# Attention's products with V as float32 products in one half of TensorE's columns

## The chip, the cores and the metric

One core of a Trainium2 chip runs the whole program. The metric is the device time of one execution in microseconds (us), median of three runs. The engines are TensorE (PE; its weight loads are listed as PEld), VectorE (DVE), ScalarE (ACT), GpSimd (POOL) and SyncE (SP), which issues most transfers.

## What is computed

Two layers of a hybrid block over 1152 tokens (1024 latent ones and 128 of context). In each layer three mixers share an input and an output projection: grouped-query attention (GQA, 6 heads), latent attention (MLA, 4 heads) and a state-space part; a squared-ReLU feed-forward part follows. The change is in the attention of both kinds:

```python
def block_attention(q, k, v, scale):
    ...
    def one_block(qblk):
        s = jnp.einsum('bqgrd,bsgd->bgrqs', qblk, k).astype(F32) * scale
        pr = jax.nn.softmax(s, axis=-1).astype(v.dtype)
        return jnp.einsum('bgrqs,bsgd->bqgrd', pr, v)
```

Heads have 64 values. A latent query reads 1152 keys (128 context keys from the cache, then its own 1024); a context query reads the 128 context keys of the request.

## The kernel before

Almost every product is made of float32r operands that are split in a high and a low part: `cp` rounds the high part (ACT), `lo` subtracts it to give the low part (DVE, or POOL for weights), and `mm` (line 69) multiplies the parts in two or three products that are added in PSUM. `tr` (line 73) transposes on TensorE.

`attn` streams 30 groups in each layer, one for each head of a block of 384 queries: 12 of MLA (three blocks, four heads), then 18 of GQA (three blocks, six heads). Blocks 0 and 1 hold three latent query tiles (`nq` = 3). Block 2 holds two latent tiles and the context tile, so its groups have nine key tiles for 256 queries and a tenth, `j` = 9, for the 128 context queries. For a group the steps are:

- `score`: scores `S` of a query tile against a third of the keys (three products for MLA, two for GQA); DVE copies them to `P` and takes the maximum (line 788), ACT makes the exponentials over 1152 keys (line 97).
- `trans`: three transposes of `P` to `pt` in PSUM, keys on the partitions; ACT rounds them to `ph` (line 65), DVE subtracts to give `pl` (line 78).
- `prod`: the stationary operand `g.V(j)` is the key tile's V, its high part in columns 0 to 63 and its low part in 64 to 127. Two products, with `ph` and then `pl` as the moving operand of 384 (or 256, or 128) columns, add to `oT` [128, 384].
- `fin1` copies `oT` to `oS`; `fin2` transposes `oS` and adds its two halves, which joins the products of V's high and low parts.

The scores of the next group are written between the products of this one. Beside this stream, `pull` issues background work at fixed points: the state-space outputs (`ssm_b`), the keys and values of GQA (`kv_gqa`, whose values are split by ACT and POOL to `VY`), the modulation (`mods`), the output projection (`out_proj`). The framework's scheduler then sets the order in each engine's queue, so the order in the source isn't the order on the engine. TensorE takes its queue in order.

One place of the kernel before already has float32 products in a part of the array: `mods` puts four products of different k side by side, 32 columns each and 512 columns of moving data (tile `m`, moving operand `raw`, stationary `cT`), in layer 0 beside GQA. A float32 product shows as two rows of MATMUL and two of LDWEIGHTS in the trace, a float32r product as one of each.

Of the kernel before, what the change touches and what calls it, by code (L numbers as in the profile page):

```python
# [4 lines left out]
F32 = mybir.dt.float32  # L5
# [8 lines left out]
L = 2  # L14
NT = 9            # token tiles: 8 latent, 1 context
NB = 3            # blocks of three token tiles
BK = 384
EPS = 1e-6
# how long (ns) background work is left alone where a chain over several engines is under way
# [3 lines left out]
# worth (ns) of background work issued at each point of the main stream  # L23
PU = (600, 850, 600, 500, 1100, 500, 400, 400, 500, 900)
SEG = [[(0, 384, 0)], [(0, 384, 0)], [(0, 256, 0), (256, 384, 1)]]
# columns of the packed small parameters
# [4 lines left out]
class Group:  # L31
    """One head of one block of queries in the attention stream."""
# [5 lines left out]
class Net:  # L38
# [7 lines left out]
    # ---------------------------------------------------------------- helpers  # L46
# [9 lines left out]
    # Rough prices (ns) of what is issued, so that background work can be paced.  # L56
# [42 lines left out]
    def rsqrt(self, v, n):  # L99
        """1/sqrt of v [128, n], by Newton's steps in float32."""  # L100
# [29 lines left out]
    # Work that runs beside the main stream: generators, advanced a step at a time.  # L130
    # One that yields a number is left alone for about so many ns.
# [7 lines left out]
    def turns(self, gens):  # L139
        """Advances the generators in the list in turn; more may be added to it meanwhile."""  # L140
        due = {}
        while gens:
            ready = [g for g in gens if due.get(g, 0) <= self.now]
            if not ready:
                g = min(gens, key=lambda g: due[g])
                yield due[g] - self.now
                ready = [g]
            for g in ready:
                try:
                    due[g] = self.now + (next(g) or 0)  # L150
                except StopIteration:
                    gens.remove(g)
                yield

    def pull(self, ns=500):
        """Issues background work worth ns of the engine that it uses most."""
# [15 lines left out]
    # ------------------------------------------------------------- modulation  # L172
    def mods(self, l, groups, engs=None, raw=None, ps=None):
        """Columns of the modulation: at the start as products, later on VectorE, with a product
        that only sums over the partitions."""
        nc = self.nc
        sums = []
        for g in groups:
# [16 lines left out]
            elif l == 0 and g < 10:  # L195
                # four products of different k side by side in the array, 32 columns each, of which two count
# [59 lines left out]
    # ------------------------------------------------------------------ norms  # L256
# [3 lines left out]
    def squares(self, sq, src, h, dve=False, eng=None):  # L260
        """Squares of the h-th quarter of src, over 1024; their sum over the features of a partition
        is in sq[:, 0] after the last one."""
# [11 lines left out]
    def stats(self, sq, out, src=None, pool=None, tag="m", bufs=2):  # L274
        """Broadcast of rsqrt(mean(src^2) + eps) over features, [128, 384] in PSUM; without src,
        the squares are there."""
# [21 lines left out]
    def prenorm(self, l, which, x, b, hi, lo, sq, squared=False):  # L298
        """x (overwritten) -> modulated h, split in hi + lo; without sq, x is normed already."""
# [19 lines left out]
    def postnorm(self, l, which, src, x, b, sq, squared=False, again=False, lazy=False):  # L319
        """x += gate * gain * rmsnorm(src); src is overwritten. again: sq gets the squares of x.  # L320
        lazy: it isn't waited for, and GpSimd does what it can."""
# [28 lines left out]
    # ------------------------------------------------------------------ build  # L350
    def build(self):
# [16 lines left out]
        # silu of the conditioning, split  # L368
        # (what follows the conditions only keeps 32 columns in reach)
# [61 lines left out]
    # ---------------------------------------------------------------- in-proj  # L431
    def in_proj(self, l, hT):
# [54 lines left out]
        # ---- group 3: kpe | z | dt  # L487
# [12 lines left out]
        # ---- x, B, C of the state-space part: feature-major, with the convolution  # L500
# [27 lines left out]
        # the first two blocks before the last one, whose norm may still be under way  # L528
# [49 lines left out]
        # ---- group 2: va | qc | kvc, and the query up-projection of MLA  # L578
# [63 lines left out]
        # ---- group 1: qa | ka; its first products run ahead of what is left of group 2  # L642
# [38 lines left out]
    def rope(self, x, C, S, nh, q, tp, eng, eng2=None):  # L681
        """x [128, nh*d] in place: x*C + partner(x)*S, d = 4q."""
# [15 lines left out]
    def ssm_steps(self, l, b, tp):  # L698
        """Softplus of the steps of a block, cumulated decays; everything [128, dir, tile, head]."""
# [19 lines left out]
        # dA = -exp(a_log) * dt  # L719
# [35 lines left out]
    # -------------------------------------------------------------- attention  # L755
    def dup_split(self, pt, hi, lo, n):
        """pt rows (x; x): hi and lo in full."""
        self.cp(hi[:, :n], pt[:, :n])
        self.lo(lo[:, :n], pt[:, :n], hi[:, :n])

    def attn(self, groups, tp, ps):
        """Streams the groups: scores of the next one run beside the products with V of this one.
        A group has b, prep() -> pairs of (stationary [128, 384], moving [128, 1280]),
        V(j) -> [128 keys, (hi | lo)], scale, dst() and done()."""
# [8 lines left out]
        def score(g, i, j):  # L773
            """Scores of query tile i against the j-th third of the keys, with their maximum."""
# [28 lines left out]
        def trans(g, j):  # L803
# [6 lines left out]
            ph = tp.tile([128, BK], R, name="ph", bufs=3)  # L810
            pl = tp.tile([128, BK], R, name="pl", bufs=3)
            self.cp(ph[:, c0:c1], pt[:, c0:c1])
            self.lo(pl[:, c0:c1], pt[:, c0:c1], ph[:, c0:c1])
            return ph[:, c0:c1], pl[:, c0:c1], c0, c1

        def prod(g, j, t):
            ph, pl, c0, c1 = t
            if j == 0:
                g.oT = ps.tile([128, BK], F32, name="oT", bufs=1)
            first, last = j in (0, 9), j in (8, 9)  # L820
            self.mm(g.oT[:, c0:c1], g.V(j), ph, first, False)
            self.mm(g.oT[:, c0:c1], g.V(j), pl, False, last)

# [23 lines left out]
        for n, g in enumerate(groups):  # L847
# [3 lines left out]
            for j in range(nj):  # L851
# [4 lines left out]
                prod(g, j, ts[j])  # L856
# [11 lines left out]
    def qT(self, src, tp, ps, name):  # L868
        """src: three [128 tokens, 128] tiles -> split transposes."""
# [8 lines left out]
    # ------------------------------------------- the three mixers  # L878
    def mix(self, l):
        """MLA (beside it the state-space outputs, then keys and values of GQA), then GQA  # L880
        (beside it the out-projection of the blocks that are done)."""
# [9 lines left out]
        # ---- keys and values of MLA  # L891
# [38 lines left out]
        V = xm.tile([128, 10, 4, 2, 64], R, name="V")  # L930
        for j in range(10):
# [6 lines left out]
            self.cp(V[:, j, :, 0, :], p3)  # L938
            self.lo(V[:, j, :, 1, :], p3, V[:, j, :, 0, :])
# [20 lines left out]
        VY = kv.tile([128, 10, 2, 2, 64], R, name="VY")  # L960
        KY = kv.tile([128, 2, 1280], R, name="KY")
        self.bg += [self.kv_gqa(l, VY, KY, ss, blk), self.ssm_b(l, ss)]

        def query(src, h, n, rep, col):
            """Head h of the block at hand, n columns repeated rep times: [128, 3, rep * n]."""
# [10 lines left out]
        for b in range(NB):  # L976
            for h in range(4):
# [22 lines left out]
                groups.append(Group(b, prep, lambda j, h=h: V[:, j, h].rearrange("p v d -> p (v d)"),  # L1000
# [10 lines left out]
        for b in range(NB):  # L1011
            for h in range(6):
# [33 lines left out]
                groups.append(Group(b, prep, lambda j, h=h: VY[:, j, h // 3].rearrange("p v d -> p (v d)"),  # L1046
# [41 lines left out]
    def ssm_a(self, l, ss):  # L1088
        """Per chunk: its state, and beside it the decayed scores (keys on the partitions)."""
# [18 lines left out]
        def front(t):  # L1108
            """The products of B and C of the chunk, both groups."""
# [524 lines left out]
```

## Time and profile before

| | |
|---|---|
| median of three runs | 3523.4 us |
| lowest and highest | 3520.69 and 3524.45 us |
| span of the profiled execution, first to last instruction | 3515.7 us |
| between span and median | 7.7 us |
| attention of layer 0, of layer 1 | about 407 to 882 us, 2160 to 2610 us |
| PE busy, DVE busy, ACT busy (share of the span) | 92%, 68%, 44% |

The attention takes about a quarter of the time. A busy engine is one that has at least one instruction under way: a matmul's duration includes its way through the array, and the next one starts long before it ends. What a matmul takes from its successors is therefore read from start to start, not from its duration. For DVE and ACT durations count.

### The profile page before, as it was taken

What the parts mean: (1) busy time and instruction counts of PE and PEld (TensorE: products, weight loads), DVE (VectorE), ACT (ScalarE), POOL (GpSimd) and SP (SyncE); (2) the same over time, 40 slices, a digit from 0 to 9 for tenths busy, and PEclk for the clock granted to TensorE, in tenths of its full rate; (3) what the DMA queues carried; (4) which work ended last, traced back from release to release, by engine and by line L of the source; (5) the groups of instructions that cost most, each with busy time, mean ns of one, the idle gap of its engine ahead of it and who ended that gap; (6) DMA issues with size and microseconds to landing.
All of it is one profiled execution on the core that took longest, in us unless ns stands there. A gap on an engine that the chain in (4) does not pass through costs nothing.

```text
span 3515.7 us, 51450 instructions
## 1 busy us (share of the span) xinstructions
PE 3229.9 (92%) x18578; PEld 3044.7 (87%) x18578; DVE 2400.3 (68%) x6199; ACT 1559.8 (44%) x3250; POOL 1279.6 (36%) x918
## 2 busy tenths in 40 slices
PE   6978799999799999999989778999887999999997
PEld 3966698788699999999989667989887999999997
DVE  7887898766666787784588878997758433333336
ACT  4454577766442211112444646787654412222223
POOL 5356432134651112112564553341446422222135
PEclk8989899999899999999999889999998999999998
DMA  5253323512322333332433533231223211111133
GB/s 205 80 172 108 113 72 107 184 49 96 125 93 82 96 96 98 95 91 78 139 120 102 169 105 108 81 98 61 80 98 103 79 49 42 43 43 43 40 105 132
DMA packets 164532, 340.77 MB, mean 97 GB/s; under 512 B 14429, under 2 KB 105909, under 8 KB 160693
## 3 DMA queue, kind: packets, MB, share of 16 engines
q1 hardware_dynamic: 161012, 335.32, 30.0%
q8 instruction: 146, 2.39, 0.3%
q10 hardware_dynamic: 3264, 2.16, 0.2%
q14 instruction: 110, 0.89, 0.1%
HBM read 280.99 MB, written 56.44 MB: 96 GB/s over the span
## 4 chain that ended last, share of the span: by engine, by line
PE 71%; DVE 20%; ACT 3%; DMA 3%; issue 2%; POOL 1%; SPq 0%; DVEq 0%; ACTq 0%; POOLq 0%
PE g L69 47%; PE S L69 5%; PE op L69 5%; PE oT L69 4%; PE pt L73 4%; DVE big L89 2%; PE m L69 2%; DVE rs_t L83 2%; PE m L73 2%; DVE cv L93 1%; DVE big L83 1%; DVE E L93 1%; DVE P L788 1%; DVE h L83 1%; DVE pl L78 1%
## 5 line engine op out<-in xcount | busy, mean ns | idle before, releaser
L78 POOL TENSOR_TENSOR w<-raw,w 128x1024 fp32r<-128x1024 f32 (+1 forms) x266 | 653.1, 2460 | 1409.3 <-ACT w L65 1365.8
L69 PE MATMUL g<-h,w 128*128 128x384 f32 x5328 | 953.6, 339 | 14.3 <-DVE h L78 12.9
L69 PEld LDWEIGHTS g<-h,w 128*128 128x128 f32 x5328 | 931.8, 189 | 17.7 <-DVE h L78 13.9
L69 PE MATMUL g<-big,w 128*128 128x384 f32 x4608 | 818.7, 336 | 13.7 <-DVE big L78 9.9
L69 PEld LDWEIGHTS g<-big,w 128*128 128x128 f32 x4608 | 800.6, 188 | 19.4 <-DVE big L78 12.0
L65 ACT CAST w<-raw 128x1024 fp32r<-128x1024 f32 (+1 forms) x266 | 275.9, 1041 | 651.6 <-PE g L69 366.1
L83 DVE TENSOR_TENSOR big<-big,g 128x384 f32<-128x384 f32 x336 | 182.9, 551 | 289.2 <-PE g L69 288.5
L83 DVE TENSOR_TENSOR r<-r 128x384 f32<-128x384 f32 x192 | 146.6, 765 | 294.3 <-ACT r L97 294.1
L69 PE MATMUL g<-w,h 128*128 128x512 f32 (+1 forms) x1296 | 320.9, 404 | 24.0 <-ACT w L65 6.1
L788 DVE TENSOR_SCALAR_CACHE_REDUCE P<-S 128x384 f32<-128x384 f32 (+1 forms) x500 | 265.9, 541 | 101.7 <-PE S L69 95.8
L69 PEld LDWEIGHTS g<-w,h 128*128 128x128 f32 x1296 | 255.7, 200 | 70.2 <-DVE h L78 6.9
L78 DVE TENSOR_TENSOR pl<-pt,ph 128x384 fp32r<-128x384 f32 (+2 forms) x560 | 270.2, 498 | 40.1 <-ACT ph L65 35.2
L65 ACT CAST ph<-pt 128x384 fp32r<-128x384 f32 (+2 forms) x560 | 233.1, 444 | 90.6 <-PE pt L73 77.6
L73 PE MATMUL pt<-cst,P 128*128 128x128 f32 x1460 | 256.1, 275 | 1.3 <-ACT P L97 0.9
L97 ACT ACTIVATE r<-g 128x384 f32<-128x384 f32 x192 | 94.3, 491 | 362.1 <-PE g L69 344.7
L93 DVE SCALAR_TENSOR_TENSOR macc<-raw,cT,macc 128x128 f32<-128x128 f32 x784 | 254.9, 389 | 0.0
L69 PE MATMUL op<-big,w 128*128 128x384 f32 x1152 | 227.1, 343 | 8.4 <-DVE big L78 8.4
L78 DVE TENSOR_TENSOR big<-r,big 128x384 fp32r<-128x384 f32 x192 | 167.7, 874 | 86.7 <-ACT big L65 86.3
L97 ACT ACTIVATE P<-P,mx 128x1152 f32<-128x1152 f32 x180 | 210.5, 1170 | 27.9 <-DVE mx L89 27.0
L69 PEld LDWEIGHTS op<-big,w 128*128 128x128 f32 x1152 | 202.8, 191 | 9.9 <-DVE big L78 9.0
L73 PEld LDWEIGHTS pt<-cst,P 128*128 128x128 f32 x1460 | 188.3, 142 | 16.8 <-issue 1.7
L65 ACT CAST big<-r 128x384 fp32r<-128x384 f32 x192 | 98.2, 512 | 185.4 <-DVE r L83 185.2
(299 smaller groups left out, 4933.9 us busy)
## 6 DMA issues: line engine op xcount, KB each, us to landing
raw<-in_w SPq DMA_DIRECT2D x176, 512.0 KB, 3.6
raw<-in_w_mod SPq DMA_DIRECT2D x80, 512.0 KB, 3.5
raw<-in_w_out SPq DMA_DIRECT2D x48, 512.0 KB, 3.6
big<-s_x SPq DMA_DIRECT2D x13, 1536.0 KB
E<-s_ac SPq DMA_DIRECT2D x36, 384.0 KB, 4.3
s_x<-big SPq DMA_DIRECT2D x9, 1536.0 KB
cv<-s_cv SPq DMA_DIRECT2D x36, 320.0 KB, 3.5
h<-in_w_mod SPq DMA_DIRECT2D x16, 512.0 KB, 9.2
```

The costliest lines, as they stand in the source:

```text
L65: self.nc.scalar.copy(out, in_)
L69: self.nc.tensor.matmul(out, lhsT=lhsT, rhs=rhs, start=start, stop=stop)
L73: self.nc.tensor.transpose(out, in_, self.ident[:p, :p])
L78: (eng or self.nc.vector).tensor_tensor(out=out, in0=src, in1=hi.bitcast(F32), op=ALU.subtract)
L83: (eng or self.nc.vector).tensor_tensor(out=out, in0=a, in1=b, op=op)
L89: (eng or self.nc.vector).tensor_scalar(out=out, in0=a, scalar1=s1, scalar2=s2, op0=op0, **kw)
L93: self.nc.vector.scalar_tensor_tensor(out=out, in0=a, scalar=s, in1=b, op0=op0, op1=op1)
L97: self.nc.scalar.activation(out=out, in_=in_, func=func, **kw)
L788: nc.vector.tensor_scalar(out=p[:, j * 384:j * 384 + nk], in0=S, scalar1=1.0, scalar2=None, op0=ALU.mult, op1=ALU.max, accum_out=mx[:, j:j ...
```

## The change

V is kept in float32, once: `V` [128, 9, 4, 64] and `VY` [128, 9, 2, 64], without a low part. The tenth key tile has a tile of its own, `V9` and `VY9`, with 64 columns of zeros beside its 64 of V, so that its product covers both halves of `oT`. `trans` copies `pt` to one float32 tile `pT` (ACT for two key tiles of three, DVE for the third) in place of the pair `ph`, `pl`. `prod` becomes `prods`: a key tile has one float32 product of 64 columns, even tiles to rows 0 to 63 of `oT`, odd tiles to rows 64 to 127, and they are written in two bursts, after the fourth transpose and at the group's end. `fin2` is the same and now adds even and odd tiles. `VY` is loaded straight from memory by three transfers on SP ahead of the stream, and `kv_gqa` no longer loads or splits V. Comments were taken out, too.

```diff
@@ trans, prod
-            ph = tp.tile([128, BK], R, name="ph", bufs=3)
-            pl = tp.tile([128, BK], R, name="pl", bufs=3)
-            self.cp(ph[:, c0:c1], pt[:, c0:c1])
-            self.lo(pl[:, c0:c1], pt[:, c0:c1], ph[:, c0:c1])
-            return ph[:, c0:c1], pl[:, c0:c1], c0, c1
-
-        def prod(g, j, t):
-            ph, pl, c0, c1 = t
-            if j == 0:
+            pT = tp.tile([128, BK], F32, name="pT", bufs=8)
+            if j % 3 == 1:
+                self.spend(2, pt[:, c0:c1], 1.04, 68)
+                nc.vector.tensor_copy(pT[:, c0:c1], pt[:, c0:c1])
+            else:
+                self.cp(pT[:, c0:c1], pt[:, c0:c1])
+            return pT[:, c0:c1], c0, c1
+
+        def prods(g, js, ts):
+            if js[0] == 0:
                 g.oT = ps.tile([128, BK], F32, name="oT", bufs=1)
-            first, last = j in (0, 9), j in (8, 9)
-            self.mm(g.oT[:, c0:c1], g.V(j), ph, first, False)
-            self.mm(g.oT[:, c0:c1], g.V(j), pl, False, last)
+            for j in js:
+                pT, c0, c1 = ts[j]
+                self.spend(0, pT, 0.9, 0)
+                r = slice(0, 128) if j == 9 else slice(64 * (j % 2), 64 * (j % 2) + 64)
+                nc.tensor.matmul(g.oT[r, c0:c1], lhsT=g.V(j), rhs=pT, start=j in (0, 1, 9), stop=j in (7, 8, 9))
@@ the loop over the key tiles
-                prod(g, j, ts[j])
+                if j == 3:
+                    prods(g, range(4), ts)
+                if j == nj - 1:
+                    prods(g, range(4, nj), ts)
@@ mix
-        V = xm.tile([128, 10, 4, 2, 64], R, name="V")
+        V = xm.tile([128, 9, 4, 64], F32, name="V")
+        V9 = xm.tile([128, 4, 2, 64], F32, name="V9")
+        nc.gpsimd.memset(V9[:, :, 1], 0.0)
...
-            self.cp(V[:, j, :, 0, :], p3)
-            self.lo(V[:, j, :, 1, :], p3, V[:, j, :, 0, :])
+            self.cp(V[:, j] if j < 9 else V9[:, :, 0], p3)
...
-        VY = kv.tile([128, 10, 2, 2, 64], R, name="VY")
+        VY = kv.tile([128, 9, 2, 64], F32, name="VY")
+        VY9 = kv.tile([128, 2, 2, 64], F32, name="VY9")
+        nc.gpsimd.memset(VY9[:, :, 1], 0.0)
+        self.dma(VY[:, 0], a["c_v"][l])
+        self.dma(VY[:, 1:9].rearrange("p t g d -> p t (g d)"), self.s_v[0:8].rearrange("t p c -> p t c"))
+        self.dma(VY9[:, :, 0], self.s_v[8].rearrange("p (g d) -> p g d", g=2))
@@ kv_gqa
-            vt = tp.tile([128, 3, 128], F32, name="zsl", bufs=2)
...
-                self.cp(V[:, j0:j1, g, 0, :], v4[:, :, g])
-                self.lo(V[:, j0:j1, g, 1, :], v4[:, :, g], V[:, j0:j1, g, 0, :], nc.gpsimd)
```

TensorE's queue in the first MLA groups of layer 0, before: each key tile has its transposes (`pt`), a product with `ph` and one with `pl`, and the scores `S` of the next group stand between them.

```order
L73 MATMUL pt<-cst,P 128x128 x3
L69 MATMUL oT<-ph,V 128x384
L69 MATMUL S<-KT,qh 128x384
L69 MATMUL S<-KT,ql 128x384
L69 MATMUL S<-KR,qq 128x384
L69 MATMUL oT<-pl,V 128x384
L73 MATMUL pt<-cst,P 128x128 x3
```

The same engine and stretch with the change (`64x384`: the product covers 64 of the array's columns):

```order
L73 MATMUL pt<-cst,P 128x128 x3
L828 MATMUL oT<-pT,V 64x384
L69 MATMUL S<-KT,qh 128x384
L69 MATMUL S<-KT,ql 128x384
L69 MATMUL S<-KR,qq 128x384
L73 MATMUL pt<-cst,P 128x128 x3
L828 MATMUL oT<-pT,V 64x384
L73 MATMUL m<-cst,qd 128x128 x3
L828 MATMUL oT<-pT,V 64x384
L73 MATMUL pt<-cst,P 128x128
```

The two products of a key tile have become one, and the bursts of the source are not in the queue: products of even and odd tiles stand apart, with transposes and scores of the whole array's width between them.

VectorE's queue in the same stretch, before: a `pl` for every key tile among the copies of the scores.

```order
L78 TENSOR_TENSOR pl<-pt,ph 128x384
L89 TENSOR_SCALAR mx<-mx 128x1
L788 TENSOR_SCALAR P,mx<-S 128x384
L78 TENSOR_TENSOR pl<-pt,ph 128x384
L788 TENSOR_SCALAR P,mx<-S 128x384
L78 TENSOR_TENSOR pl<-pt,ph 128x384
L83 TENSOR_TENSOR y<-y,m 128x384
```

And with the change:

```order
L813 COPY pT<-pt 128x384
L788 TENSOR_SCALAR P,mx<-S 128x384
L841 RECIPROCAL rs<-rs 128x3
L788 TENSOR_SCALAR P,mx<-S 128x384 x2
L813 COPY pT<-pt 128x384
L793 TENSOR_REDUCE mx<-mx 128x1
L89 TENSOR_SCALAR mx<-mx 128x1
L788 TENSOR_SCALAR P,mx<-S 128x384 x2
L813 COPY pT<-pt 128x384
```

Three key tiles in nine leave a copy on this engine, the other six leave nothing.

## Rows read from the trace of the kernel before

**Rows 1.** The page: busy time by engine, and the chain that ended last.

```profile
PE 3229.9 (92%) x18578; PEld 3044.7 (87%) x18578; DVE 2400.3 (68%) x6199; ACT 1559.8 (44%) x3250; POOL 1279.6 (36%) x918
PE 71%; DVE 20%; ACT 3%; DMA 3%; issue 2%; POOL 1%; SPq 0%; DVEq 0%; ACTq 0%; POOLq 0%
```

**Rows 2.** Stretches: length, busy PE, PEld, DVE, ACT, POOL, granted clock, DMA.

```profile
431.00:547.00 116.00, 115.76 (x781) 106.19 (x780) 105.92 (x368) 92.79 (x214) 35.88 (x39) 1.00 0.27 78
...
2354.00:2417.00 63.00, 62.48 (x417) 56.23 (x416) 60.46 (x221) 54.16 (x116) 3.84 (x7) 1.00 0.09 27
700.00:900.00 200.00, 178.68 (x1113) 169.05 (x1112) 121.84 (x397) 118.16 (x252) 85.87 (x52) 0.95 0.24 78
2450.00:2640.00 190.00, 168.83 (x1046) 158.88 (x1045) 114.14 (x361) 112.00 (x240) 84.03 (x51) 0.95 0.28 91
```

**Rows 3.** PE's waits from 406 to 900 us: total, times, longest.

```profile
PE S L69 <- DVE P L788: 14.6, 11, 5.1
...
PE oT L69 <- DVE pl L78: 1.4, 4, 0.5
```

**Rows 4.** DVE's costliest groups, 2183.5 to 2299.5 us: busy, mean ns, idle before.

```profile
L78 DVE TENSOR_TENSOR pl<-pt,ph 128x384 fp32r<-128x384 f32 (+2 forms) x74 | 38.2, 529 | 3.5 <-ACT ph L65 3.2
L788 DVE TENSOR_SCALAR_CACHE_REDUCE P<-S 128x384 f32<-128x384 f32 (+1 forms) x70 | 37.7, 542 | 3.1 <-PE S L69 2.2
```

**Rows 5.** PE's instructions in order of time near 640 us: start, us, what.

```profile
639.30 0.33 PE L69 MATMUL S<-KY,ql 128*128 128x384 f32 x1
639.48 0.33 PE L69 MATMUL S<-KY,qh 128*128 128x384 f32 x1
639.65 0.34 PE L69 MATMUL S<-KY,ql 128*128 128x384 f32 x1
639.92 1.91 PE L69 MATMUL m<-raw,cT 128*32 128x512 f32 x12
641.76 0.44 PE L69 MATMUL oT<-ph,VY 128*128 128x384 f32 x1
```

**Rows 6.** The same view near 645 us.

```profile
644.70 1.05 PE L69 MATMUL m<-raw,cT 128*32 128x512 f32 x4
645.68 0.45 PE L69 MATMUL S<-KY,qh 128*128 128x384 f32 x1
645.96 0.34 PE L69 MATMUL S<-KY,ql 128*128 128x384 f32 x1
```

**Rows 7.** The same view: two transposes after such products, and two elsewhere.

```profile
628.13 0.44 PE L73 MATMUL pt<-cst,P 128*128 128x128 f32 x2
...
2404.80 0.38 PE L73 MATMUL pt<-cst,P 128*128 128x128 f32 x2
```

**Rows 8.** The same view: products of 256 and of 128 columns.

```profile
840.56 0.28 PE L69 MATMUL oT<-pl,VY 128*128 128x256 f32 x1
840.68 0.28 PE L69 MATMUL oT<-ph,VY 128*128 128x256 f32 x1
...
845.34 0.22 PE L69 MATMUL oT<-ph,VY 128*128 128x128 f32 x1
845.40 0.39 PE L69 MATMUL S<-KY,qh 128*128 128x384 f32 x1
```

**Rows 9.** Weight loads (PEld) in order of time near 640 us.

```profile
639.92 0.16 PEld L69 LDWEIGHTS m<-raw,cT 128*32 128x32 f32 x8 [0.25 <-issue]
640.37 0.12 PEld L69 LDWEIGHTS m<-raw,cT 128*32 128x32 f32 x2 [0.30 <-issue]
```

**Rows 10.** All groups by line and form: `ph` products and their count.

```profile
L69 PE MATMUL oT<-ph,VY 128*128 128x384 f32 x216 | 86.8, 402 | 0.6 <-ACT ph L65 0.6
...
L69 PE MATMUL oT<-ph,V 128*128 128x384 f32 x144 | 56.6, 393 | 0.0
```

**Rows 11.** ACT in order of time, ahead of layer 0's attention.

```profile
399.13 3.61 ACT L65 CAST V<-k 128x256 fp32r<-128x256 f32 x10
402.70 1.41 ACT L65 CAST KR<-k 128x384 fp32r<-128x384 f32 x4
```

More of the change, by code (lines that the diff above doesn't have):

```diff
@@ L959, in mix @@
         blk = {}
-        VY = kv.tile([128, 10, 2, 2, 64], R, name="VY")
+        VY = kv.tile([128, 9, 2, 64], F32, name="VY")
[4 more added lines that the diff above has]
+        self.dma(VY9[:, :, 0], self.s_v[8].rearrange("p (g d) -> p g d", g=2))
         KY = kv.tile([128, 2, 1280], R, name="KY")
-        self.bg += [self.kv_gqa(l, VY, KY, ss, blk), self.ssm_b(l, ss)]
+        self.bg += [self.kv_gqa(l, KY, ss, blk), self.ssm_b(l, ss)]
         def query(src, h, n, rep, col):
@@ L998, in done @@
                         self.dma(self.s_o[3 * b:3 * b + 3, :, 0:256].rearrange("t p c -> p t c"), blk["ob"])
-                groups.append(Group(b, prep, lambda j, h=h: V[:, j, h].rearrange("p v d -> p (v d)"),
+                groups.append(Group(b, prep, lambda j, h=h: V[:, j, h] if j < 9 else V9[:, h].rearrange("p v d -> p (v d)"),
                                     96.0 ** -0.5, dst, done, PU[3]))
@@ L1044, in done @@
                     blk["oo"] = oh, ol
-                groups.append(Group(b, prep, lambda j, h=h: VY[:, j, h // 3].rearrange("p v d -> p (v d)"),
+                groups.append(Group(b, prep, lambda j, h=h: VY[:, j, h // 3] if j < 9 else VY9[:, h // 3].rearrange("p v d -> p (v d)"),
                                     0.125, dst, done, PU[4]))
@@ L1320, in ssm_b, with kv_gqa @@
             yield from second(t)
-    def kv_gqa(self, l, V, KT, tp, blk):
+    def kv_gqa(self, l, KT, tp, blk):
         nc, a = self.nc, self.a
@@ L1326, in kv_gqa @@
             kt = tp.tile([128, 3, 128], F32, name="zsl", bufs=2)
-            vt = tp.tile([128, 3, 128], F32, name="zsl", bufs=2)
-            for z, cache, scr in ((kt, "c_k", self.s_qk[:, :, 384:512]), (vt, "c_v", self.s_v)):
-                f = 1 if j0 == 0 else 0
-                if f:
-                    self.dma(z[:, 0], a[cache][l].rearrange("p g d -> p (g d)"))
-                self.dma(z[:, f:n], scr[j0 + f - 1:j1 - 1].rearrange("t p c -> p t c"))
+            f = 1 if j0 == 0 else 0
+            if f:
+                self.dma(kt[:, 0], a["c_k"][l].rearrange("p g d -> p (g d)"))
+            self.dma(kt[:, f:n], self.s_qk[j0 + f - 1:j1 - 1, :, 384:512].rearrange("t p c -> p t c"))
             yield D[4]
-            v4 = vt[:, :n].rearrange("p t (g d) -> p t g d", d=64)
             for g in range(2):
-                self.cp(V[:, j0:j1, g, 0, :], v4[:, :, g])
-                self.lo(V[:, j0:j1, g, 1, :], v4[:, :, g], V[:, j0:j1, g, 0, :], nc.gpsimd)
                 kd = tp.tile([128, 3, 2, 64], F32, name="xt", bufs=2)
```

## The prediction

> **What bounds the kernel now.** I read the page's shares first. TensorE is busy 92% of the span and carries 71% of the chain that ended last, DVE 20% [rows 1]; that is an average over stages, and the change lies in one of them. So I read busy time by stretch within the attention. In a stretch of MLA groups PE is busy 115.76 of 116 us, DVE 105.92, ACT 92.79; in GQA groups of layer 1 that have little beside them PE has 62.48 of 63, DVE 60.46; the later GQA groups, beside the output projection, leave PE some idle time: 21.3 of 200 us in layer 0, 21.2 of 190 in layer 1 [rows 2]. The view of waits agrees: in 494 us of layer 0's attention PE waits 14.6 us for score copies on DVE, 11 times, once for 5.1, and 1.4 us for `pl` [rows 3]. So PE is the bound, at its full granted clock (1.00), with DVE close behind. A cheaper DVE can give back only PE's idle time, and whatever PE gains or loses in the products moves the end. The sum is therefore made on PE. It is made as an addition to the profiled execution (span 3515.7 us) and applied to the median, 3523.4, which lies 7.7 above that span.
>
> **What the products cost now.** From start to start, float32r products of 384 columns follow each other in 0.17 us (639.30 to 639.65 for two [rows 5]; I use 0.174), those of 256 columns in 0.12 and those of 128 in 0.06 [rows 8]. There are 360 `ph` products of 384 columns [rows 10] (40 groups of three latent tiles, nine key tiles), 180 of 256 and 20 of 128 from block 2, and as many with `pl`. On PE that is 720 x 0.174 + 360 x 0.12 + 40 x 0.06 = 125 + 43 + 2 = 170 us.
>
> **What a float32 product costs.** The trace has float32 products in a part of the array: the modulation's, 32 columns wide with 512 columns of moving data. Four MATMUL rows are two products in two column groups: from their start to the next instruction's 0.98 us pass (644.70 to 645.68 [rows 6]). Twelve rows are six products, of which four fit side by side, so two rounds: 1.84 us (639.92 to 641.76 [rows 5]). The second round cost 0.86 us, 1.68 ns a column: four times a float32r product's 0.174 / 384 = 0.45. Products side by side in different columns share a round. With the round's price taken in proportion, a round of 384 columns costs 0.645 us, of 256 0.43, of 128 0.215. That 64 columns cost what 32 cost is my choice; the time follows the moving data here.
>
> **How many rounds.** A product shares a round only if its neighbour in PE's queue uses the other half, and the queue is taken in order. The source writes bursts, but in the built order the products stand in 424 runs: 312 of one, 92 of two (always an even and an odd tile), 16 of three, 4 of four. Counted by width, with an even-odd pair as one round, that gives 295 rounds of 384 columns, 134 of 256 and 20 of 128 (the tenth tiles, which take the whole width): 295 x 0.645 + 134 x 0.43 + 20 x 0.215 = 190 + 58 + 4 = 252 us.
>
> **What the switches cost.** A run is preceded and followed by instructions over all 128 columns. Going in: from the start of a score product to the start of the narrow one 0.27 us pass in place of 0.17 (639.65 to 639.92 [rows 5]), 0.10 more. Coming out: the round of 0.98 us is 0.12 more than 0.86 [rows 6], and the first wide instruction then holds up the second: a score product by 0.11 (645.68 to 645.96, 0.28 in place of 0.17 [rows 6]), a transpose by 0.06 (two transposes take 0.44 in place of 0.38 [rows 7]). In the built order 410 runs contain a narrow product (14 are a tenth tile alone); after about 70% of these a transpose follows, otherwise mostly scores. A run thus pays 0.10 + 0.12 + 0.08 = 0.30 us, and 410 pay 123 us. Bounds: 0.22 if PE stood idle before most runs, 0.36 if the wider weights add as much again as the narrow ones seem to.
>
> The second pass's weights are loaded while the first pass runs: eight loads stand within 0.16 us of 639.92, two for each of four products, and the next two at 640.37, ahead of a round that starts about 0.43 later [rows 9]. The Trainium skill (TensorE: Matmul & The Clock Gate, Part 3, The mechanism) says that a weight load overlaps running matmuls only when it goes to other row groups, and these use all rows. By that rule each of some 860 passes would show its load, at an estimated 0.055 us for 64 columns (half of the 0.11 that a full-width load shows after a switch), 47 us more; by the row it costs nothing, and the trace doesn't agree with the rule.
>
> **The other engines.** DVE loses 560 subtractions of some 0.53 us each in the stretch shown [rows 4] and gets 180 copies; I find no copy of this form in the rows and bound it by zero and the 0.54 of the score copy from PSUM [rows 4]. Either way DVE ends far below PE. ACT loses 180 of 560 roundings. What this buys is at most PE's idle time: about 42 us in the two late stretches [rows 2] and the 14.6 us of waits in layer 0, taken twice [rows 3], of which hardly any is for `pl`. I take 10 us, bounds 0 and 42. Leaving out the splitting of MLA's V gains nothing: ACT casts V until 402.70 and only then the last key part `KR`, which the first scores need [rows 11]; ACT's copies remain, so DVE's earlier end is hidden behind them. The three loads of `VY` stand on SP ahead of a load of queries and the loads of keys; what they bring is needed only by the GQA groups, more than 150 us later, and the query load is the one thing queued behind them that is soon wanted: nothing, bound 4 us a layer. Clearing the zero halves on POOL is off the path.
>
> **Sum.** 252 + 123 - 170 = +205 on PE, less 10 = +195: 3523.4 + 195 = 3718, say **3715 us**. For a group of three latent tiles this is +3.7 us, for one of block 2 +2.8, 60 groups in all. Ends: 252 + 0.22 x 410 - 170 - 42 = +130 (3653), and with no product sharing a round (360 x 0.645 + 180 x 0.43 + 4 = 314) and the dear switch 314 + 148 - 170 = +292 (3815).
>
> **Rivals.** Four ways in which it could go otherwise.
> 1. All even and odd products share rounds after all, because the halves work on their own queues and wait for nothing between. Then rounds cost 314 / 2 = 157 us, and 157 + 123 - 170 - 10 = +100: 3623. Against it: no wide instruction starts before the narrow round's end in [rows 5, 6], and narrow and wide instructions alternate in the queue. If instead the bursts ran as written, a group would have five rounds and two runs: 5 x 0.645 + 0.60 = 3.83 against 18 x 0.174 = 3.13, some +0.7 for each of 60 groups, 3565; the built order excludes it. The Trainium skill (TensorEngine Tiling (Array Packing), Theoretical Speedup) gives up to 2x for an operand of 64 columns or fewer; that is this rival, and the rows bear it out only for neighbours in the queue. Chance 5%.
> 2. Halves of 64 columns don't run side by side as the 32-column groups do: 314 in place of 252, 3780. Nothing in the rows speaks for it, but none shows 64. Chance 7%.
> 3. New waits on PE: there is one `oT`, so a group's first product waits until `oS` has been copied; with products now last in the group's work this wait, under 1 us in a group, may show: 60 x 0.5 to 1 = 30 to 60 us more, 3745 to 3775. For it: longer products that are followed directly by the copy. Against it: PE hardly waits for `ph` or `pl` now [rows 3], and scores and transposes of the next group stand between. Chance 10%; the rule on weight loads, another 4%, lands at 3762.
> 4. Faster: DVE and ACT, not PE, set the pace of the groups, and PE's longer products fill time in which it only seems busy. This decides from the point where the products' whole price, now put at 375 us, falls below 170 plus the idle time that DVE can give back, at most 42 + 29: about 240, less than the rounds alone. If the switches cost nothing and the rounds 230, the time would be 3523 + 230 - 170 - 71 = 3512. For it: DVE is at 91% and 96% in [rows 2]. Against it: PE is at 99% there, and the waits of rows 3 are short. Chance 3%.
>
> **How the numbers follow.** The forecast has 70%, the rivals 5, 7, 10 + 4 and 3%, and 1% is left for no change. The range is 3640 to 3800: it takes in the forecast's cheap end, rivals 2 and 3 and most of the dear end, and leaves out rivals 1 and 4 and the far dear corner. A measurement of this kernel can tell about 0.2% (7 us) from no change: faster 3%, same 1%, slower 96%.
>
> **What would show it.** In the changed kernel: MATMUL rows of `oT` should be two for each product, with starts 0.32 us apart for 384 columns; the step into a run 0.10 and out of it 0.12 above the bare time; pairs of different halves should start together. PE should be busy over 98% of the groups, with DVE falling to about half, and a GQA group of three tiles in layer 1 should take about 14 us in place of about 10.5 (63 us for six groups [rows 2]). The feed-forward stage should be unchanged. I am wrong if the passes of 64 columns cost other than 0.32 us, if runs drain for more or less than 0.3 us, or if PE shows idle time in front of the products.

## Result and the profile after

The changed kernel takes 3716.61 us (median of 4 runs, 3714.54 to 3720.03), the kernel before, beside it, 3522.05 (4 runs, 3518.35 to 3524.45). The ratio is 1.0558, with a 95% interval of 1.0545 to 1.057: slower by 195 us. The span of the profiled execution went from 3515.7 to 3715.7 us.

The page of the changed kernel, the rows that answer to [rows 1]: busy time by engine, the chain that ended last by engine, and the same chain by line.

```profile
PE 3425.0 (92%) x18578; PEld 2960.8 (80%) x18578; DVE 2274.6 (61%) x5799; ACT 1498.6 (40%) x3054; POOL 1266.3 (34%) x906
PE 74%; DVE 16%; DMA 3%; ACT 2%; issue 2%; POOL 2%; SPq 0%; DVEq 0%; ACTq 0%; POOLq 0%
PE g L69 44%; PE oT L828 8%; PE S L69 6%; PE pt L73 5%; PE op L69 4%; PE m L69 2%; PE m L73 2%; DVE big L89 2%; DVE rs_t L83 2%; DVE big L83 2%; DVE cv L93 1%; DVE E L93 1%; PE k L69 1%; POOL big L83 1%; PE mod_q L69 1%
```

PE issues the same number of instructions, 18578, and is busy 195 us longer; DVE, ACT and POOL all have less to do. The products with V, now one line of their own (`oT`, line 828), are 8% of the chain.

Where the time went is read by stage. The stretches are the two attentions (first score to last product), before and after, with length, busy PE, PEld, DVE, ACT, POOL, granted clock, DMA share and GB/s. First the kernel before:

```profile
406.80:881.50 474.70, 449.87 (x2940) 403.70 (x2940) 368.12 (x1278) 335.36 (x740) 150.29 (x129) 0.98 0.33 103
2159.90:2609.50 449.60, 429.22 (x2795) 395.79 (x2796) 363.44 (x1258) 330.33 (x727) 150.86 (x129) 0.98 0.26 81
```

And the changed kernel, with what follows the second attention as a third stretch:

```profile
405.50:980.40 574.90, 552.94 (x2935) 361.90 (x2936) 305.55 (x1092) 305.84 (x642) 145.86 (x123) 0.97 0.27 85
2266.50:2797.10 530.60, 515.82 (x2791) 347.59 (x2792) 303.58 (x1072) 299.43 (x630) 146.72 (x123) 0.99 0.22 68
...
2797.10:3715.70 918.60, 860.56 (x4890) 852.17 (x4889) 380.68 (x572) 258.23 (x419) 297.85 (x129) 0.96 0.22 70
```

The attention grew by 100.2 and 81.0 us, together 181, at nearly the same granted clock (0.98 and 0.98 before, 0.97 and 0.99 now). The other 19 us of the profiled span are outside it. DVE lost 63 and 60 us of work in the same stretches, and the time did not fall by it.

How a run of products now stands in PE's queue. The view lists PE's instructions in order of time (start, us, what) in a GQA group of layer 1, changed kernel:

```profile
2687.24 0.87 PE L73 MATMUL pt<-cst,P 128*128 128x128 f32 x6
2688.04 1.50 PE L828 MATMUL oT<-pT,VY 128*64 128x384 f32 x6
2689.48 0.87 PE L73 MATMUL pt<-cst,P 128*128 128x128 f32 x6
2690.28 0.86 PE L828 MATMUL oT<-pT,VY 128*64 128x384 f32 x2
2691.07 0.55 PE L73 MATMUL pt<-cst,P 128*128 128x128 f32 x3
2691.55 0.87 PE L828 MATMUL oT<-pT,VY 128*64 128x384 f32 x4
2692.34 0.44 PE L73 MATMUL pt<-cst,P 128*128 128x128 f32 x2
```

Two rows of MATMUL are one product. A single product (x2) holds the queue for 0.79 us from its start to the next instruction's, an even-odd pair (x4) for 0.79 as well, three products (x6) for 1.44. So a pair shares one round, a round is 0.645 and each run adds about 0.15. Before, the two products of a key tile cost 2 x 0.174 = 0.35 us.

All runs of the trace, counted from start to start, give the price in full. The products hold PE for 321 us; 252 of it is the rounds of the prediction, and 69 is what each of the 424 runs adds to its rounds, its drain (0.16 each; two waits of over 4 us in all are among the 69, and without them it is 0.15). The steps into the runs add 43.5 us (0.10 each), and the second wide instruction behind a run is late by 30 us in all (0.07 each). That is 394 us where the kernel before has 173. Of the difference of 221 us, 79 is rounds and 142 is switches.

### The profile page after: what moved, and what is told of

The parts are those of the page before. It is cut to its first block, busy times and chain, and to the rows that moved or that the text cites. A ratio compares the mean times of both kernels' runs of the same rounds, so it can differ in the third digit from the quotient of the medians.

```text
span 3715.7 us, 50418 instructions
## 1 busy us (share of the span) xinstructions
PE 3425.0 (92%) x18578; PEld 2960.8 (80%) x18578; DVE 2274.6 (61%) x5799; ACT 1498.6 (40%) x3054; POOL 1266.3 (34%) x906
## 4 chain that ended last, share of the span: by engine, by line
PE 74%; DVE 16%; DMA 3%; ACT 2%; issue 2%; POOL 2%; SPq 0%; DVEq 0%; ACTq 0%; POOLq 0%
PE g L69 44%; PE oT L828 8%; PE S L69 6%; PE pt L73 5%; PE op L69 4%; PE m L69 2%; PE m L73 2%; DVE big L89 2%; DVE rs_t L83 2%; DVE big L83 2%; DVE cv L93 1%; DVE E L93 1%; PE k L69 1%; POOL big L83 1%; PE mod_q L69 1%
## 5 line engine op out<-in xcount | busy, mean ns | idle before, releaser
L73 PEld LDWEIGHTS pt<-cst,P 128*128 128x128 f32 x1460 | 171.1, 142 | 157.6 <-issue 115.3
L65 ACT COPY pT<-pt 128x384 f32<-128x384 f32 (+2 forms) x380 | 159.7, 437 | 183.6 <-PE pt L73 182.4
L828 PE MATMUL oT<-pT,VY 128*64 128x384 f32 (+2 forms) x672 | 208.8, 475 | 0.0
```

What stands on the lines that cost most here:

```text
L65: self.nc.scalar.copy(out, in_)
L73: self.nc.tensor.transpose(out, in_, self.ident[:p, :p])
L828: nc.tensor.matmul(g.oT[r, c0:c1], lhsT=g.V(j), rhs=pT, start=j in (0, 1, 9), stop=j in (7, 8, 9))
```

## Experiments

The theory is the prediction's: PE's price is made of rounds and of switches, and both follow from the order in the queue. Two rivals stand against it: that the switches are cheap and the float32 products themselves dear, and that the order doesn't matter at all, because something else (a wait, the way through PSUM) sets the pace; the expectations give these rivals their own times. All the kernels but E5, E9 and E10 are edits of the changed kernel. A ratio is always to the kernel before, run beside it; "attention" is the sum of both layers in the profiled run. "Narrow runs" are those with a product of 64 columns: 410 of the 424, since 14 are a tenth tile alone. The price on PE is counted as above; for the float32r products of the kernel before and of E5 it is the bare one.

| | narrow runs | products on PE, us | attention | outside | median of runs | ratio and interval |
|---|---|---|---|---|---|---|
| before | | 173 | 924.3 | 2591.4 | 3522.05 | |
| after | 410 | 394 | 1105.5 | 2610.3 | 3716.61 | 1.0558 (1.0545 to 1.057) |
| E1 whole bursts | 128 | 223 | 944.7 | 2612.6 | 3558.19 | 1.0097 (1.0082 to 1.0112) |
| E2 one burst | 71 | 205 | 950.9 | 2603.5 | 3555.39 | 1.0096 (1.0081 to 1.0111) |
| E3 full width | 0 | 327 | 1045.1 | 2595.0 | 3647.92 | 1.0353 (1.0337 to 1.0368) |
| E5 no `pl` | | 173 | 922.5 | 2591.2 | 3520.67 | 0.9997 (0.9987 to 1.0006) |
| E6 evens, then odds | 68 | 277 | 1021.3 | 2608.9 | 3629.9 | 1.0306 (1.0289 to 1.0322) |
| E7 one half | 336 | 434 | 1132.3 | 2593.3 | 3727.47 | 1.0589 (1.0571 to 1.0606) |
| E8 split tile | 75 | 193 | 945.0 | 2602.7 | 3552.65 | 1.0089 (1.0074 to 1.0104) |
| E9 more buffers | | | 931.0 | 2603.7 | 3530.99 | 1.0028 (1.0017 to 1.0039) |
| E10 bursts of the kernel before | | | 957.7 | 2589.6 | 3551.39 | 1.0087 (1.0071 to 1.0102) |

**E1, the bursts as they are written.** I took it that the scheduler had taken the bursts apart because their first product was ready first. If the product whose operand is ready last stands first, nothing can slip in between.

```diff
-            for j in js:
+            for j in [j for j in js if j < 9][::-1] + [j for j in js if j == 9]:
...
-                nc.tensor.matmul(g.oT[r, c0:c1], lhsT=g.V(j), rhs=pT, start=j in (0, 1, 9), stop=j in (7, 8, 9))
+                nc.tensor.matmul(g.oT[r, c0:c1], lhsT=g.V(j), rhs=pT, start=j in (3, 2, 9), stop=j in (5, 4, 9))
```

> The changed kernel with one edit: a burst's products are written from the last key tile to the first, so that all are ready when the first of them is and the built order keeps the bursts whole: 128 narrow runs in place of 410, and rounds worth 176 us in place of 250. Theory (PE is the bound; rounds of 1.67 ns a column, and every run pays for a switch in and out, about 0.33 us as the changed kernel's trace shows): PE's price of the products falls from 394 us to 176 + 128 x 0.33 = 218, so 3717 - 176 = 3540 us, still a little slower than before. Rival A (switches are cheap, only unshared rounds count): 74 us less, about 3640. Rival B (the time went into new waits of the groups, not into PE's work): within 40 us of 3717.

PE in order of time in E1:

```profile
431.18 0.34 PE L69 MATMUL S<-KR,qq 128*128 128x384 f32 x1
431.44 2.15 PE L828 MATMUL oT<-pT,V 128*64 128x384 f32 x10
433.52 0.55 PE L73 MATMUL pt<-cst,P 128*128 128x128 f32 x3
```

Five products (x10) take 2.08 us: three rounds of 0.645 and 0.15. In the source nothing but the order of the same products was changed, and 158 of the 195 us are gone. That excludes the rivals at 3640 and 3717. The miss: 3558 instead of 3540. The attention came to within 20 us of the kernel before; the other 21 us lie outside it, where nothing was edited.

**E2, one burst a group.** All products at the group's end, with eleven `pT`, last tile first as in E1.

```diff
-            pT = tp.tile([128, BK], F32, name="pT", bufs=8)
+            pT = tp.tile([128, BK], F32, name="pT", bufs=11)
...
-                if j == 3:
-                    prods(g, range(4), ts)
                 if j == nj - 1:
-                    prods(g, range(4, nj), ts)
+                    prods(g, range(nj), ts)
```

> All products of a group in one burst at the group's end, last key tile first (eleven pT buffers): 71 narrow runs, rounds worth 175 us. Theory: 175 + 71 x 0.33 = 198 us, 196 less than the changed kernel: 3520 us, about the time before. Rival A (switches cheap): as with two whole bursts, about 3640. Rival B: a burst of 3.3 us holds up the next group's scores and its end waits for the copy of oT, so that it is slower than with two whole bursts by 0.5 us or more a group, 30 us: 3570.

PE in order of time in E2:

```profile
429.31 0.34 PE L69 MATMUL S<-KR,qq 128*128 128x384 f32 x1
429.58 3.44 PE L828 MATMUL oT<-pT,V 128*64 128x384 f32 x18
432.95 0.44 PE L73 MATMUL pt<-cst,P 128*128 128x128 f32 x2
```

Nine products (x18) take 3.37 us, five rounds of 0.645 and 0.15: the price was as expected, and 18 us on PE cheaper than E1's. The time is E1's (3555 against 3558, their ranges overlap), not the 3520 expected: the attention, 950.9 us, is even 6 us longer than E1's. Nearly half of E1's narrow runs are gone and the time did not follow. Against the kernel before, E1 is charged 50 us more on PE and its attention grew by 20; E2 is charged 32 and grew by 27. So E2's attention has some 24 us more of other gaps on PE than E1's. Whether one long burst fills less of the idle time that is there, or makes waits of its own as rival B had it (3570), was not told apart.

**E3, full width.** Each key tile's V stands beside 64 columns of zeros, and its product covers all 128 columns. There is no narrow product left, and no round is shared.

```diff
-                r = slice(0, 128) if j == 9 else slice(64 * (j % 2), 64 * (j % 2) + 64)
+                r = slice(0, 128)
...
-        V = xm.tile([128, 9, 4, 64], F32, name="V")
+        V = xm.tile([128, 9, 4, 2, 64], F32, name="V")
+        nc.gpsimd.memset(V[:, :, :, 1], 0.0)
...
```

> The changed kernel with V of every key tile beside 64 columns of zeros, as its tenth tile has it: 560 float32 products over all 128 columns, no even and odd halves, so no switch and no shared round; written as in the changed kernel. Theory: rounds of the same price whatever the width, 311 us, no switches: 394 - 311 = 83 us less than the changed kernel, 3634 us. Rival A (switches are cheap): 61 us more than the changed kernel, 3777. Rival C (a pass takes as long as its columns are many): rounds twice as long, over 3900.

PE in order of time in E3:

```profile
426.56 0.49 PE L73 MATMUL pt<-cst,P 128*128 128x128 f32 x3
426.88 1.46 PE L828 MATMUL oT<-pT,V 128*128 128x384 f32 x4
428.18 0.49 PE L73 MATMUL pt<-cst,P 128*128 128x128 f32 x3
```

3648 lies by the 3634 expected, far below the 3777 and the 3900 of the rivals. Two products take 1.30 us, 0.65 each: a pass costs the same with 128 columns as with 64, and no drain of 0.15 us is added before the transposes. The kernel does twice the array's work of the changed one per product, shares nothing, and is 69 us faster. In this order the halves cost more in switches than they save in rounds.

**E7, one half only.** E3 with tiles 1 to 7 narrow again, all in the same half. Nothing can share a round, so against E3 only the switches are added.

```diff
-                r = slice(0, 128)
+                r = slice(0, 128) if j in (0, 8, 9) else slice(0, 64)
-                nc.tensor.matmul(g.oT[r, c0:c1], lhsT=g.V(j), rhs=pT, start=j in (0, 9), stop=j in (8, 9))
+                nc.tensor.matmul(g.oT[r, c0:c1], lhsT=g.V(j)[:, :128 if j in (0, 8, 9) else 64], rhs=pT, start=j in (0, 9), stop=j in (8, 9))
```

> As the kernel with full-width float32 products (V beside zeros), but key tiles 1 to 7 in the first half only, without the zeros; tiles 0, 8 and 9 stay full. No two products share a round in either kernel, and rounds are worth 311 us in both; only the width and with it the switches differ: 336 narrow runs in place of none. Theory: 336 x 0.33 = 111 us more than 3648: 3759. Rival A (switches are cheap): within 20 us of 3648. Rival (narrow passes are shorter): below 3648.

PE in order of time in E7:

```profile
427.91 0.49 PE L73 MATMUL pt<-cst,P 128*128 128x128 f32 x3
428.33 1.50 PE L828 MATMUL oT<-pT,V 128*64 128x384 f32 x4
429.76 0.55 PE L73 MATMUL pt<-cst,P 128*128 128x128 f32 x3
```

The same two products, narrow, take 1.43 us in place of 1.30, and the transposes lie 0.42 us ahead of them instead of 0.32. The price on PE rises by 107 us, 0.32 for each of the 336 runs, near the 0.335 of the changed kernel; the time rises by 80 (3727 against 3648; 3759 was expected), the profiled attention by 87. So the switch has the price expected, and 20 us of it lay in idle time of the attention: the gaps of 0.4 us or more on PE are 14 us shorter than in E3. The rival, for which the switch is free, had 3648.

**E6, evens and then odds.** E2 with the order 8, 6, 4, 2, 0, 7, 5, 3, 1. If a product must wait for all ahead of it in the queue, only the last even and the first odd tile can share a round: eight rounds in place of five.

```diff
-            for j in [j for j in js if j < 9][::-1] + [j for j in js if j == 9]:
+            for j in (8, 6, 4, 2, 0, 7, 5, 3, 1, 9)[:len(js)]:
```

> As the kernel with one burst a group, but within the burst first the products of all even tiles (one half of the columns), then those of all odd ones: 68 narrow runs in place of 71, the same products. Only neighbours differ. Theory (a product shares a round only with a neighbour in PE's queue): rounds worth 278 us in place of 175, 103 us more than the 3555 of one burst: 3658. Rival 1 of the prediction (the halves have queues of their own): no change, 3555.

PE in order of time in E6:

```profile
427.39 0.34 PE L69 MATMUL S<-KR,qq 128*128 128x384 f32 x1
427.65 4.79 PE L828 MATMUL oT<-pT,V 128*64 128x384 f32 x18
432.37 0.44 PE L73 MATMUL pt<-cst,P 128*128 128x128 f32 x2
```

The same nine products take 4.72 us: seven rounds and 0.20, neither five nor eight. Sharing depends on the neighbours in the queue, as the prediction said, with one product of grace (see the last section). The time, 3630, lies between the 3658 expected and the rival's 3555; it rises by 74.5 us over E2, the price on PE by 72.

**E8, the ninth tile.** Nine tiles are five rounds with one half empty in the last. Tile 7 is cut by queries, half of it in each half of the columns, and the other eight are dealt out anew, four to each half; otherwise E2.

```diff
-            for j in js:
+            for j in (8, 6, 7, 5, 4, 3, 2, 1, 0, 9)[:len(js)]:
...
+                if j == 7:
+                    m = c1 // 2
+                    nc.tensor.matmul(g.oT[0:64, 0:m], lhsT=g.V(j), rhs=pT[:, 0:m], start=False, stop=False)
+                    nc.tensor.matmul(g.oT[64:128, m:c1], lhsT=g.V(j), rhs=pT[:, m:c1], start=False, stop=False)
+                    continue
...
```

> As the kernel with one burst a group, but the product of the odd one of nine key tiles (tile 7 here) is cut in two by columns of queries, one part for each half, so that the halves carry equal loads: 4.5 rounds a group in place of 5. Rounds worth 162 us in place of 175, 75 narrow runs in place of 71. Theory: 12 us less than 3555: 3543, still slower than before by some 20. Rival B (the burst's waits count, not PE's work): no change, 3555.

3552.65 against E2's 3555.39: the price on PE fell by 12 us as expected, the profiled attention by 6 and the median by 3, where the two ratios' intervals overlap. That misses the theory (3543) and lies nearer to the rival (3555): at most half of what PE saved reached the time, while E6, with bursts as whole, shows that work added on PE does. It is the fastest of the float32 versions and some 32 us above the kernel before.

**E5, what the cheaper DVE is worth.** The kernel before, with `ph` used twice.

```diff
-            pl = tp.tile([128, BK], R, name="pl", bufs=3)
             self.cp(ph[:, c0:c1], pt[:, c0:c1])
-            self.lo(pl[:, c0:c1], pt[:, c0:c1], ph[:, c0:c1])
-            return ph[:, c0:c1], pl[:, c0:c1], c0, c1
+            return ph[:, c0:c1], ph[:, c0:c1], c0, c1
```

> The kernel before without the subtraction that makes pl; the second product of a key tile uses ph again, so the low part of the probabilities is left out of the result and PE's work is the same. It measures what relief of DVE alone (560 subtractions, about 280 us of DVE) is worth. Theory (PE is the bound, DVE gives back PE's idle time only): 10 to 40 us faster, about 3500. Rival (DVE sets the pace of the groups): 100 us faster or more, 3420 or less.

The two attentions of E5, columns as above:

```profile
404.70:880.50 475.80, 449.90 (x2935) 405.17 (x2935) 267.03 (x998) 333.04 (x739) 149.66 (x129) 0.97 0.32 103
2158.80:2605.50 446.70, 423.92 (x2790) 394.64 (x2791) 265.26 (x978) 328.22 (x727) 150.37 (x129) 0.97 0.28 85
```

DVE does 199 us less in the attention, and the time is the same within 0.1%. I had expected at least 10 us. PE's longest wait is unmoved; here is the view of waits in E5, layer 0 (total, times, longest), which answers to [rows 3]:

```profile
PE S L69 <- DVE P L788: 15.4, 11, 5.5
```

So the waits for score copies don't come from DVE's load, and the idle time that DVE could give back is nothing.

**E9 and E10, the kernel before in bursts.** E9 has four `ph` and `pl` in place of three; E10 uses them to write three key tiles' six products together, `pl` first, so as to save PE the changes between products and scores.

```diff
-                prod(g, j, ts[j])
+                if j % 3 == 2 or j == 9:
+                    for i in [9] if j == 9 else [j, j - 1, j - 2]:
+                        prod(g, i, ts[i])
...
```

> The kernel before with four ph and four pl buffers in place of three each; nothing else. It is the control for the next run, and shows how much the time outside the attention moves when only the built order moves. Theory: attention within 5 us of the kernel before, the rest within 20: 3505 to 3540.

> The kernel before, float32r products over all columns as before, but three key tiles at a time, the last one first and pl ahead of ph, so that the built order has runs of six products (175 of them) where it had mostly single ones; four ph and four pl buffers. Theory from the starts in the trace of before: its 1120 products take about 200 us of PE with the steps into them, 173 at their bare price; in whole runs most of the 27 should go: 15 to 25 us less, about 3500. Rival: between instructions of the same width order costs nothing, 3521.

PE in order of time in E10:

```profile
429.74 0.27 PE L73 MATMUL pt<-cst,P 128*128 128x128 f32 x1
430.51 0.45 PE L69 MATMUL oT<-pl,V 128*128 128x384 f32 x1 [0.49 <-DVE pl L78]
430.79 0.34 PE L69 MATMUL oT<-ph,V 128*128 128x384 f32 x1
430.97 0.33 PE L69 MATMUL oT<-pl,V 128*128 128x384 f32 x1
```

E9 is 9 us slower and E10 29 us slower than the kernel before; the theory that bursts as such save time falls. Inside the burst, after its first product, they follow each other at the old 0.17 to 0.18 us, so there is no gain, and the burst's first product waits for a `pl` (0.49 us here). By the view of waits PE waits for `pl` for 14 us in both layers, before for 3. The 27 us that the expectation took for steps are not steps. The kernel before, in order of time:

```profile
2387.45 0.49 PE L73 MATMUL pt<-cst,P 128*128 128x128 f32 x3
2387.69 0.42 PE L69 MATMUL oT<-ph,VY 128*128 128x384 f32 x1
2387.95 0.34 PE L69 MATMUL oT<-pl,VY 128*128 128x384 f32 x1
2388.13 0.49 PE L73 MATMUL pt<-cst,P 128*128 128x128 f32 x3
```

Three transposes and two products take 0.68 us, their bare price (3 x 0.11 and 2 x 0.174). Over its 784 runs of products, counted with the steps on both sides, the median lies 0.006 us above the bare price and three in four lie under 0.02; what there is more stands in some 170 places, most of them under 0.4 us. So there was no step for bursts to save. E9 shows something else: its profiled span has 12 us more outside the attention, where nothing was edited, and 7 within it (at most 5 were expected). None of the versions beats the kernel before; E5, which leaves out the low part of the probabilities, equals it.

## Why the prediction was right

The forecast was 3715 us and the result 3716.6, on the mechanism named. That they are so close is luck, for errors of the sum cancel. The prediction had +205 on PE, -10 for idle time and 0 outside the attention. The profiled spans, 200.0 us apart, have +221, -40 (what is left in the attention) and +19.

**PE is the bound: right.** PE's products grew and the time grew; DVE's relief, in E5 by itself, changed nothing.

**Rounds: right.** MATMUL rows of one product are 0.32 us apart, 0.37 in the first product of a run (0.05 of the run's drain stands there), and pairs start together. E3 adds that the price does not depend on the columns. The kernel before can be set at 173 us where the prediction had 170.

The second pass's weights cost nothing here either. The changed kernel, a single product (PE rows) and its weights (the PEld row):

```profile
2605.59 0.86 PE L828 MATMUL oT<-pT,VY 128*64 128x384 f32 x2
2606.38 2.35 PE L69 MATMUL op<-big,w 128*128 128x384 f32 x12
...
2605.59 0.19 PEld L828 LDWEIGHTS oT<-pT,VY 128*64 128x64 f32 x2 [0.25 <-issue]
```

Both loads end at 2605.78, while the first pass still runs: its successor starts at 2605.96. By the rule in the Trainium skill (TensorE: Matmul & The Clock Gate, Part 3, The mechanism), that a load overlaps running matmuls only when the row groups differ, the second could not have been hidden; here again the trace doesn't agree with that rule, though the text ahead of it also allows a load into a background weight buffer.

**Switches: mis-sized by some 0.03 us.** Predicted 0.10 in, 0.12 and 0.08 out, 0.30 for each of 410 runs; measured 0.10, 0.16 (0.15 without the two waits) and 0.07 over all 424, 142 us in place of 123. The step out of the run, taken from one row of four 32-column products, was the short one. E7 against E3 gives 0.32 with nothing else changed in the source.

**Idle time: mis-sized, and for another reason.** The prediction took 10 us, with a bound of 42, and argued from what a cheaper DVE could give back. E5 shows that DVE gives back nothing. What happened is that PE's longer products took up gaps that were there before. Counted from start to start beyond each instruction's bare time, the other gaps on PE were 120 us in both attentions of the kernel before, 120 in E5 and 86 in the changed kernel. Of the 34 us less, 13 are in gaps of 0.4 us or more, the rest in short ones, which the busy share doesn't show, because a matmul's duration covers them: PE was busy 449.87 of 474.70 us. The prediction went by the idle time of that view alone. E7 shows the same a second time, with 107 us on PE and 87 in the attention. What each short gap waits for was not tried, and the other 6 of the 40 us are not accounted for.

**Outside the attention: predicted 0, measured +19.** 10 us are in the two seams between the last products and the feed-forward part, 10 in the feed-forward parts; the rest cancels. One such place is the first feed-forward chunk after the second attention. The changed kernel, PE in order of time:

```profile
2918.46 15.13 PE L69 MATMUL g<-big,w 128*128 128x384 f32 x72 [4.26 <-ACT big L65]
```

A wait of 4.3 us for ACT, where the kernel before has two for ACT that sum to 0.8. The 20 us around it, first changed, then before (columns as above):

```profile
2904.70:2924.70 20.00, 14.40 (x66) 13.80 (x66) 17.57 (x17) 9.07 (x15) 15.80 (x7) 0.83 0.46 157
```

```profile
2712.10:2732.10 20.00, 18.25 (x104) 17.17 (x103) 16.20 (x21) 10.92 (x18) 13.47 (x6) 1.00 0.46 158
```

PE is idle for 5.6 us in place of 1.8, and the mean granted clock is 0.83 in place of 1.00: within the wait it falls from 2.4 to 1.2 GHz for a part of the stretch. In the nine experiments this outside part varies between -2 and +21 us, +12 in E9 where only a buffer count differs. It doesn't follow the products' price (+4 in E3, +2 in E7, +21 in E1). That it comes from the order that the scheduler builds is argued, not shown.

**Signs.** DVE at about half: 305.55 of 574.90 and 303.58 of 530.60, right. PE over 98% in the groups: 96% and 97% over the attention, a little less than I said. A GQA group of three tiles in layer 1, from the last product of one to that of the next, for six in a row: 11.6 to 15.6 us, mean 14.2, where the kernel before has 10.5, right. The copy that had no row before costs DVE 0.55 us (0.54 was the bound):

```profile
L813 DVE COPY pT<-pt 128x384 f32<-128x384 f32 x120 | 66.4, 554 | 43.0 <-PE pt L73 42.3
```

**Rivals.** Rival 1, that the halves share without regard to order, falls by E6, but for one product (see the last section); its second half, the bursts as written at 3565, is E1 at 3558. What the prediction held against it reads [rows 5, 6] too strictly: the wide instruction does start 0.07 us before the narrow rows end, by the ends that the profile gives. Rival 2 (no sharing at 64 columns) falls by the pairs. Rival 3, new waits on `oS`: the view of waits shows none, and PE waits less for scores than before, in layer 0 (against [rows 3]) and in layer 1:

```profile
PE S L69 <- DVE P L788: 12.6, 7, 3.3
```

```profile
PE S L69 <- DVE P L788: 9.8, 7, 3.8
```

Rival 4, DVE as the pace, falls by E5.

## What to carry to other kernels

Before putting products into a part of the array, count in the built order how often the queue goes from narrow to wide: here each such run cost a third of a microsecond whatever its length, and the order of the source said nothing of it. To keep a burst whole under a scheduler, write the product first whose operand is ready last. And find the slack of the bounding engine from start to start, and ask what would fill it: the longer products took up 34 us of gaps on a PE that was busy for 95% of the time, and a relief of 199 us on the next engine was worth nothing.

## What the runs showed of the hardware

**A product of the free half can pass one that stands ahead of it.** In E6's queue, in the order built, stand five even products and then four odd ones. The trace doesn't name the half of a row. The starts of the eighteen passes of the run shown, in us (worked out from the trace):

```
427.654 428.027 428.350 428.672 428.995 429.317
429.640 429.646   429.962 430.020   430.285 430.342   430.607 430.665
430.987 431.310 431.632 431.955
```

Eight passes stand in four pairs, from the seventh on. The six passes ahead of them, three even products, follow each other at 0.32 us, so products of one half don't pair, and the first odd product starts beside the fourth even one, 0.64 us before the fifth, which is ahead of it in the queue. Strict order would have paired only the fifth and made 16 slots; there are 14. The Trainium skill (TensorE: Matmul & The Clock Gate, Part 3, The mechanism) says that MATMULs keep strict program order in start and end; for the two halves of the columns this run doesn't agree. It is one product of grace, not a free queue: but for that, TensorE takes its queue in order, as the description of the kernel says. The run shown takes 4.72 us, as nearly all whole runs of 384 columns do.

**The float32 pass has one price.** 0.32 us for 384 columns of moving data, whether 64 columns of the array take part (the starts above, after the first) or 128 (E3), so a narrow product saves nothing by being narrow; only a neighbour in the other half does.
